# A two-layer hybrid encoder on one core: when the first weight sums of the FFN are made, who adds the squares of the norms, and what is fetched or kept for the last down projections

## The chip, the cores and the metric

The kernel runs on one core of a Trainium2 chip. The metric is the device time of one execution in microseconds (us), as the median of several runs. Engines are named as in the profile: PE multiplies matrices (its weight loads are PEld), DVE, ACT and POOL work element by element, SP issues transfers. Each engine works through its own list of instructions in order, so an instruction that waits holds up all that stand behind it on that engine. A transfer issued by POOL can add into its destination instead of overwriting it; such a one is called an adding DMA here.

## The reference

Two layers over 768 tokens of 1024 channels (256 of a prompt and 512 of a sample). Each layer is a norm, three token mixers, gates and an output projection, then a second norm and a gated FFN of 2816 channels, both with a residual:

```python
h = x + mixers(rmsnorm(x, norm1_g)) @ w_out
up = rmsnorm(h, norm2_g) @ w_up                  # 2 x 2816 columns
up = centred depthwise conv of width 3 over tokens(up)
x = h + (silu(gate half of up) * value half of up) @ w_down
```

After the second layer there is a last rmsnorm. `rmsnorm(x, g)` is `x * rsqrt(mean(x*x) + eps) * g`, with the mean over the 1024 channels of one token. All is float32.

## The kernel before

Activations lie with channels on the 128 partitions and 768 tokens along the row, as 8 tiles (m = 0 to 7) for 1024 channels. Every float32 product is three PE products of rounded parts: hi*hi, hi*lo, lo*hi. For weights, ACT makes the hi part `wh` (L320, L330) and DVE the lo part `wl` by subtracting (L349). `Stream` (object `W`) walks through a fixed list of weights and issues loads, hi and lo parts some steps ahead of their use.

**The norm is applied late.** `prep` and `layer_out` write the unnormalized values times g. The factor of a token, `rsqrt`, is found beside the products: `sumsq(x, k)` squares tile k on ACT (L487, L490) and adds it to one accumulator page, tiles 1 to 6 on POOL and 7 on DVE (both L492). `rstd_tok` sums over partitions on PE (L498, 12 products), scales on DVE (L501) and takes the power on POOL (L504). `rstd_bc` spreads the factors over all partitions: small diagonal matrices on DVE (L518), products on PE (L519), copies on ACT (L521).

**`layer_out`** computes the output projection tile by tile ("out m"). DVE adds the residual (L988) to the PSUM buffer, ACT and DVE make the hi and lo parts of three combinations for the FFN (L970, L968, L971, L991 to L998), `sumsq` follows, and POOL stores the tile to `x_mid` (L1002).

**The FFN up projection** works on 22 groups g of 128 gate and 128 value columns. Each is a two by two block product in 7 pieces instead of 8 (P1 to P7; products at L1092 into the PSUM buffers `ga` and `gb`, copies out at L1100 to L1116). Some pieces multiply sums of weight quarters `qa` to `qd`. Those sums are adding DMAs on POOL (`add`, L272): sum1 is qc += w, sum2 is qd += qc, sum3 is qb += w, sum4 is raw += qd. `load2` asks SP for qd. `Stream.acts` says at which piece each is issued, counted from the group's P1; for g = 0 the negative counts fall into the last outs. P2 of a group needs qd after sum2. The convolution, silu and product of a group (L1029 to L1072) run over the pieces that follow.

**The down projections** ("dn") take the 22 blocks in 8 chunks c0 to c7 of 2 or 3 (FFC), each for 8 tiles m. `ffn_steps` writes one order of pieces and dn steps; `TAIL` dn steps of the next to last chunk stay for after the last piece. A dn is `dense` (L425) into one of two PSUM buffers d (`dps` takes turns), then `evac`: DVE adds the residual page that SP fetched from DRAM (L1152), SP stores it. In chunk c7 of layer 0, `evac` also calls `prep` (ACT L478, DVE L479) and `sumsq` for the next layer. In layer 1, c7 is computed in two cuts of columns (512, then 256) with the weights loaded and split twice; its evacuation is L1142, and `final` then scales (L1210) and stores.

**`dense_tok`** (L538) computes a mixer's input projection with tokens on partitions: tiles 0 to 3 lie in d buffer 0, tiles 4 and 5 in buffer 1. The first one of a layer (`kouter`) runs in two halves s = 0, 1 over the channels, and in s = 0 with the channel block outside and all 6 tiles inside. Its copy out is L570 on ACT.

Pages of 128x768 come from a pool of 7 and are free again when their last reader is done.

## Time and profile before

| | |
|---|---|
| median of 3 runs | 2481.14 us (2477.6 to 2487.31) |
| profiled execution | 2487.01 us, of which the span is 2485.2 us |
| mean granted clock of PE in the span | 0.985 |
| PE busy | 2400.7 us |
| DVE busy | 1549.1 us |
| ACT busy | 1110.7 us |
| POOL busy | 297.8 us |

In a row of the trace's timeline the numbers are start (us from the span's start) and duration, then engine, line, operation, what is written and read, and in brackets how long the engine was idle before it and what it is held to have waited for. A granted clock of 1.00 means that PE ran at the higher of its two levels (2.4 GHz) throughout the stretch, 0.50 that it ran at the lower (1.2 GHz).

### The profile page before, as it was taken

The numbers are of one execution on the slowest core, as the hardware profiler recorded it, in microseconds if no ns is written. First come the engines' busy times: TensorE is split into PE (matmuls) and PEld (weight loads), VectorE is DVE, ScalarE is ACT, GpSimd is POOL, SyncE is SP. The second block draws the span as 40 slices with busy tenths as digits, with TensorE's granted clock in tenths as the row PEclk, the third lists the DMA queues.
The fourth block names the chain that finished last, engine by engine and source line by source line (L and its number), as shares of the span: only waits on it lengthen the run. The fifth ranks groups of instructions, "written<-read, shape, count | busy, mean of one in ns | idle before, by whom it ended". The sixth has DMA issues, their size and how long they took to land. (4 is left out here: it accounts for less than half of the span.)

```text
span 2485.2 us, 38816 instructions
## 1 busy us (share of the span) xinstructions
PE 2400.7 (97%) x15030; PEld 2325.9 (94%) x15030; DVE 1549.1 (62%) x2689; ACT 1110.7 (45%) x2194; POOL 297.8 (12%) x406
## 2 busy tenths in 40 slices
PE   9999999999989999999799999999999899999996
PEld 8999999899979999999799999998999899999995
DVE  5555446554648777777745554555446687777775
ACT  4344345652335444444423553466323454444442
POOL 1000110000221111111100001100003211111102
PEclk9999999999989999999999999999999999999998
DMA  4411321113358987887622113111124698878854
GB/s 146 101 58 50 53 69 52 35 35 101 123 125 228 258 239 223 229 229 211 198 86 64 50 50 71 60 43 35 43 104 136 134 271 248 241 216 245 223 168 159
DMA packets 140712, 336.12 MB, mean 135 GB/s; under 512 B 16616, under 2 KB 35176, under 8 KB 140528
## 3 DMA queue, kind: packets, MB, share of 16 engines
q1 hardware_dynamic: 109296, 265.99, 32.6%
q0 software_dynamic: 31232, 67.66, 15.3%
q8 instruction: 118, 1.93, 0.3%
q14 instruction: 66, 0.54, 0.1%
HBM read 251.79 MB, written 58.72 MB: 125 GB/s over the span
## 5 line engine op out<-in xcount | busy, mean ns | idle before, releaser
L425 PE MATMUL d<-u,wh 128*128 128x384 f32 (+2 forms) x4608 | 1024.4, 343 | 17.1 <-DVE u L1142 7.9
L425 PEld LDWEIGHTS d<-u,wh 128*128 128x128 f32 x4608 | 806.7, 189 | 37.2 <-issue 26.4
L425 PE MATMUL d<-u,wl 128*128 128x384 f32 (+2 forms) x2304 | 596.7, 338 | 0.0
L425 PEld LDWEIGHTS d<-u,wl 128*128 128x128 f32 x2304 | 421.0, 189 | 1.1
L349 DVE TENSOR_TENSOR wl<-raw,wh 128x512 fp32r<-128x512 f32 (+1 forms) x261 | 256.6, 985 | 199.0 <-ACT wh L330 159.8
L1092 PE MATMUL ga<-u,wh 128*128 128x384 f32 x1408 | 364.9, 340 | 11.7 <-ACT u L1100 7.9
L1092 PE MATMUL gb<-u,wh 128*128 128x384 f32 x1056 | 274.5, 341 | 15.7 <-ACT u L970 7.8
L1092 PEld LDWEIGHTS ga<-u,wh 128*128 128x128 f32 x1408 | 256.9, 189 | 14.5 <-ACT u L1100 8.7
L538 PE MATMUL d<-wh,u 128*128 128x256 f32 x1344 | 250.2, 286 | 11.0 <-DVE pg L1152 7.7
L1092 PE MATMUL ga<-u,wl 128*128 128x384 f32 x704 | 238.8, 339 | 0.1
L538 PEld LDWEIGHTS d<-wh,u 128*128 128x128 f32 x1344 | 212.6, 193 | 13.2 <-issue 8.0
L1092 PEld LDWEIGHTS gb<-u,wh 128*128 128x128 f32 x1056 | 193.1, 190 | 18.5 <-ACT u L970 8.4
L538 PE MATMUL d<-wl,u 128*128 128x256 f32 x672 | 191.7, 285 | 3.0 <-DVE wl L349 3.0
L330 ACT ACTIVATE wh<-raw 128x1024 fp32r<-128x1024 f32 x129 | 135.3, 1049 | 109.3 <-PE d L538 52.1
L1092 PE MATMUL gb<-u,wl 128*128 128x384 f32 x528 | 179.1, 339 | 0.0
L1152 DVE TENSOR_TENSOR pg<-d,pg 128x768 f32<-128x768 f32 x120 | 114.6, 955 | 85.9 <-PE d L425 80.8
L1029 ACT ACTIVATE pg<-u,vec 128x769 f32<-128x769 f32 x88 | 91.0, 1034 | 111.4 <-DVE u L1037 76.3
L1092 PEld LDWEIGHTS ga<-u,wl 128*128 128x128 f32 x704 | 133.3, 189 | 0.7 <-DVE wl L349 0.7
L538 PEld LDWEIGHTS d<-wl,u 128*128 128x128 f32 x672 | 129.2, 192 | 3.6 <-DVE wl L349 3.4
L636 DVE TENSOR_TENSOR u<-s,u 128x128 fp32r<-128x128 f32 (+1 forms) x112 | 36.9, 329 | 121.1 <-ACT u L635 120.9
L1092 PEld LDWEIGHTS gb<-u,wl 128*128 128x128 f32 x528 | 100.1, 190 | 0.1
L731 PE MATMUL s<-u,u 128*128 128x256 f32 (+2 forms) x384 | 99.9, 342 | 0.0
(191 smaller groups left out, 3129.1 us busy)
## 6 DMA issues: line engine op xcount, KB each, us to landing
raw<-w_pk SPq DMA_DIRECT2D x174, 512.0 KB, 3.7
pg<-xm SPq DMA_DIRECT2D x120, 384.0 KB, 5.1
xm<-pg SPq DMA_DIRECT2D x112, 384.0 KB, 3.9
u<-w_pk SPq DMA_DIRECT2D x104, 192.0 KB, 3.4
qa<-w_pk SPq DMA_DIRECT2D x44, 256.0 KB, 4.6
qb<-w_pk SPq DMA_DIRECT2D x44, 256.0 KB, 3.1
qc<-w_pk SPq DMA_DIRECT2D x44, 256.0 KB, 3.7
qd<-w_pk SPq DMA_DIRECT2D x44, 256.0 KB, 4.4
```

The lines of the kernel that those rows point to most:

```text
L330: ACT.activation(hi[:, :n], t[:, :n], AF.Copy)
L349: DVE.tensor_tensor(lo, t, fl(hi), ALU.subtract)
L425: PE.matmul(out=ps[:, h, 0:b - a], lhsT=w, rhs=x[:, a:b], start=first and i == 0 and pi == 0, stop=last and i == nk - 1 and pi == 2,)
L538: PE.matmul(out=outs[t], lhsT=x, rhs=w, start=k == 0 and pi == 0 and t % 2 == 0, stop=k == KD - 1 and pi == 2, skip_group_check=True)
L636: DVE.tensor_tensor(u[:, 1, a:b], ps, fl(u[:, 0, a:b]), ALU.subtract)
L731: PE.matmul(out=ps[:, 0:w], lhsT=q, rhs=kb[:, c, lo * P:hi * P], start=c == 0, stop=c == 1)
L1029: ACT.activation(f, h[:, 1:770], AF.Identity, scale=cw(1, ct), bias=vec[:, VCB + ct:VCB + ct + 1])
L1092: PE.matmul(out=o, lhsT=a[:, w], rhs=x[:, b], start=p in ("P1", "P2", "P5") and kp == 0 and pi == 0, stop=kp == 3 and pi == 2, skip_group_ ...
L1152: DVE.tensor_tensor(h2(xa), ps[:, :, 0:384], h2(xa), ALU.add)
```

## The change

Seven edits: (1) all four quarters of group 0 are loaded at the start of `layer_out`, and sum1 and sum2 of group 0 are issued there; for later groups load2, sum1, sum2 and sum4 come one or two pieces earlier, with two buffers for qd. (2) For all norms but the first of the kernel, `sumsq` keeps two accumulators (even and odd tiles), adds squares 2 to 5 by adding DMAs, 6 and 7 on DVE, and joins the accumulators on DVE at k = 6. (3) `rstd_tok` comes one piece later, `rstd_bc` two. (4) One dn of the next to last chunk goes to just before the last group's P4. (5) After the last piece, residual pages are asked for two tiles ahead instead of one. (6) The lo and hi weights of layer 1's last chunk stay on chip for its second cut. (7) `dense_tok` with `kouter` takes the d buffers in turn and does tiles 0 to 3 first, then 4 and 5.

```diff
-TAIL = 4
+TAIL = 5
@@ ffn_steps
     for g, p in seq:
+        if (g, p) == (NJ - 1, "P4"):
+            r.append(("dn", todo[0][0], todo.pop(0)[1], (0, HT, T)))
         r.append(("pc", g, p))
@@ Stream.__init__
-                    for k, f in ((-2, self.load2), (-2, self.sum1), (-1, self.sum2), (0, self.sum3), (4, self.sum4)):
-                        at = j + k if e[2] == 0 and k < 0 else pcs[i + k]
-                        self.acts.setdefault(at, []).append((f, e[1], e[2]))
+                    for k, f in ((-4, self.load2), (-3, self.sum1), (-2, self.sum2), (0, self.sum3), (3, self.sum4)):
+                        if e[2] or k >= 0:
+                            self.acts.setdefault(pcs[i + k], []).append((f, e[1], e[2]))
@@ Stream.quart
-            t = ph["sb"].tile([P, 512], F32, tag="q" + k, name=nm("q" + k))
+            t = ph["sb"].tile([P, 512], F32, tag="q" + k, name=nm("q" + k), bufs=2 if k == "d" else 1)
@@ Stream.split
-                if self.open is None:
+                if e[:3] == ("down", DEPTH - 1, len(FFC) - 1):
+                    k = None
+                    if e[3] % 2 == 0:
+                        st["keep"] = unit()
+                    h, l2 = (st["keep"][:, e[3] % 2, i * HT:i * HT + w] for i in range(2))
+                elif self.open is None:
@@ sumsq
-    def sumsq(x_ap, k, dve=False):
+    def sumsq(x_ap, k, dve=None):
         n = x_ap.shape[-1]
-        if k == 0:
-            st["acc"] = page()[:, 0:n]
-            ACT.activation(st["acc"], x_ap, AF.Square)
+        c = k % 2 if dve is None else 0
+        if k == c:
+            st["acc", c] = page()[:, 0:n]
+            ACT.activation(st["acc", c], x_ap, AF.Square)
+            return
+        sq = page()[:, 0:n]
+        ACT.activation(sq, x_ap, AF.Square)
+        if dve is not None or k >= KD - 2:
+            (POOL if dve is False else DVE).tensor_tensor(st["acc", 0], st["acc", 0], sq, ALU.add)
+            if dve is None and k == KD - 2:
+                DVE.tensor_tensor(st["acc", 0], st["acc", 0], st.pop(("acc", 1)), ALU.add)
         else:
-            sq = page()[:, 0:n]
-            ACT.activation(sq, x_ap, AF.Square)
-            eng = DVE if dve or k == KD - 1 else POOL
-            eng.tensor_tensor(st["acc"], st["acc"], sq, ALU.add)
+            POOL.dma_start(out=st["acc", c], in_=sq, accum_op=ALU.add)
@@ dense_tok
-        d = [dps(0), dps(1)]
+        d = [dps(), dps()] if kouter else [dps(0), dps(1)]
...
-                order = [(kk, t) for kk in range(4) for t in range(NT)]
+                order = [(kk, t) for ts in (range(4), range(4, NT)) for kk in range(4) for t in ts]
@@ layer_out
-        W.quart("a", l)
-        W.quart("b", l)
-        W.quart("c", l)
+        for k in "abcd":
+            W.quart(k, l)
...
         fetch(1)
+        W.sum1(l, 0)
+        W.sum2(l, 0)
@@ layer_ffn
-                if s[1] == 0 and s[2] == "P6":
+                if (s[1], s[2]) == (0, "P5"):
                     rstd_tok()
-                elif s[1] == 0 and s[2] == "P7":
+                elif (s[1], s[2]) == (1, "P1"):
                     rstd_bc(gap=True)
                 elif s[1] == NJ - 1 and s[2] == "P3":
+                    deep = 3
...
-            for _, c2, m2, _ in downs[0:2]:
+            for _, c2, m2, cuts2 in downs[0:deep]:
```

The order of instructions shows the first place on DVE, at out 7 of layer 0: the addition of out 7's residual into `u` and, ahead of it, the lo part of group 0's `qd`. Before:

```order
L971 SCALAR_TENSOR_TENSOR u_6615<-u_6180,vec_91,u_6615 128x384
L992 TENSOR_TENSOR pg_6618<-pg_6616 128x384
L971 SCALAR_TENSOR_TENSOR u_6615<-pg_6618,u_6615 128x384
L349 TENSOR_TENSOR wl_6692<-qd_6619,wh_6691 128x512
L988 TENSOR_TENSOR u_6180<-d_6694,u_6180 128x768
```

The same place in the changed kernel (line numbers there are 8 to 17 higher: L504 and L506 are the two additions of `sumsq`, L357 is L349, L1005 is L988):

```order
L988 SCALAR_TENSOR_TENSOR u_6618<-u_6182,vec_91,u_6618 128x384
L1009 TENSOR_TENSOR pg_6621<-pg_6619 128x384
L988 SCALAR_TENSOR_TENSOR u_6618<-pg_6621,u_6618 128x384
L504 TENSOR_TENSOR pg_6258<-pg_6258,pg_6686 128x768
L506 TENSOR_TENSOR pg_6258<-pg_6258,pg_6326 128x768
L357 TENSOR_TENSOR wl_6692<-qd_6177,wh_6691 128x512
L1005 TENSOR_TENSOR u_6182<-d_6694,u_6182 128x768
```

Two additions (of out 6's square and of the odd accumulator) have come in ahead of out 7's residual; the odd accumulator is the one into which the last adding DMA, of out 5, goes. The second place is POOL from out 5 of layer 0 to the power of `rstd_tok` (L504 before, L520 after), with the stores of the outs (`xm`) and the sums. Before:

```order
L492 TENSOR_TENSOR pg_6254<-pg_6254,pg_6609 128x768
L1002 DMA xm_210<-u_6179 128x768
L272 DMA qc_6175<-w_pk 128x512
L492 TENSOR_TENSOR pg_6254<-pg_6254,pg_6686 128x768
L1002 DMA xm_211<-u_6180 128x768
L272 DMA qd_6619<-qc_6175 128x512
L1002 DMA xm_212<-u_6180 128x768
L1018 MEMSET u_6762 128x2 x3
L1018 MEMSET u_6766 128x2 x3
L272 DMA qb_6173<-w_pk 128x512
L504 TENSOR_TENSOR sm_6836<-sm_6834,neghalf 128x6
```

After (L508 is the adding DMA of `sumsq`, L274 a weight sum):

```order
L508 DMA pg_6326<-pg_6612 128x768
L1019 DMA xm_210<-u_6181 128x768
L1019 DMA xm_211<-u_6182 128x768
L1019 DMA xm_212<-u_6182 128x768
L1035 MEMSET u_6762 128x2 x3
L1035 MEMSET u_6766 128x2 x3
L274 DMA qb_6173<-w_pk 128x512
L274 DMA qc_6781<-w_pk 128x512
L274 DMA raw_6504<-qd_6177 128x512
L274 DMA qd_6790<-qc_6781 128x512
L520 TENSOR_TENSOR sm_6857<-sm_6855,neghalf 128x6
```

Group 0's sum1 and sum2 are gone from here (they stand at the start of the output projection), and three more sums now stand ahead of the power: sum1 and sum2 of group 1 and sum4 of group 0. The third place is DVE in the last chunk of layer 0, at m = 6 and m = 7, each with its residual (L1152 before, L1168 after) and its scaled tile (L479, L489). Before:

```order
L1152 TENSOR_TENSOR pg_11654<-d_11688,pg_11654 128x768
L479 SCALAR_TENSOR_TENSOR u_11712<-pg_11654,vec_11368,u_11712 128x768
L349 TENSOR_TENSOR wl_11719<-raw_11294,wh_11718 128x1024
L1152 TENSOR_TENSOR pg_11683<-d_11721,pg_11683 128x768
L479 SCALAR_TENSOR_TENSOR u_11745<-pg_11683,vec_11368,u_11745 128x768
L492 TENSOR_TENSOR pg_11523<-pg_11523,pg_11748 128x768
```

After:

```order
L1168 TENSOR_TENSOR pg_11624<-d_11687,pg_11624 128x768
L489 SCALAR_TENSOR_TENSOR u_11711<-pg_11624,vec_11368,u_11711 128x768
L504 TENSOR_TENSOR pg_11525<-pg_11525,pg_11714 128x768
L506 TENSOR_TENSOR pg_11525<-pg_11525,pg_11558 128x768
L357 TENSOR_TENSOR wl_11719<-raw_11283,wh_11718 128x1024
L1168 TENSOR_TENSOR pg_11655<-d_11721,pg_11655 128x768
L489 SCALAR_TENSOR_TENSOR u_11745<-pg_11655,vec_11368,u_11745 128x768
L504 TENSOR_TENSOR pg_11525<-pg_11525,pg_11748 128x768
```

The two additions of tile 6 stand ahead of tile 7's residual, where POOL added before.

## Rows read from the trace of the kernel before

**Rows 1.** The page, busy us (share of the span) and instructions of an engine.

```profile
PE 2400.7 (97%) x15030; PEld 2325.9 (94%) x15030; DVE 1549.1 (62%) x2689; ACT 1110.7 (45%) x2194; POOL 297.8 (12%) x406
```

**Rows 2.** Stretch, us; busy us of PE, PEld, DVE, ACT, POOL; granted clock; DMA.

```profile
680.00:720.00 40.00, 29.80 (x147) 28.22 (x146) 18.11 (x31) 12.21 (x23) 11.55 (x18) 0.83 0.43 105
...
1200.00:1250.00 50.00, 38.18 (x216) 37.04 (x215) 31.53 (x30) 19.88 (x26) 12.33 (x8) 0.90 0.69 223
...
1900.00:1950.00 50.00, 40.15 (x218) 38.26 (x217) 23.50 (x39) 16.32 (x29) 13.45 (x20) 0.90 0.51 127
```

**Rows 3.** Waits of PE over the span: us in total, times, longest.

```profile
PE d L425 <- DVE u L1142: 7.9, 6, 2.6
PE ga L1092 <- ACT u L1100: 7.9, 2, 4.1
PE gb L1092 <- ACT u L970: 7.8, 2, 4.0
PE d L538 <- DVE pg L1152: 7.7, 1, 7.7
```

**Rows 4.** DVE, ACT and POOL at layer 0's FFN start: start, us, instruction, [idle before].

```profile
693.71 0.69 DVE L349 TENSOR_TENSOR wl<-qd,wh 128x512 fp32r<-128x512 f32 x1 [7.07 <-ACT wh L320]
694.32 0.95 DVE L988 TENSOR_TENSOR u<-d,u 128x768 f32<-128x768 f32 x1
...
678.49 0.83 ACT L490 ACTIVATE pg<-u 128x768 f32<-128x768 f32 x1
...
693.05 0.63 ACT L320 ACTIVATE wh<-qd 128x512 fp32r<-128x512 f32 x1 [6.25 <-DMA qd<-qc]
...
701.58 0.47 ACT L1100 ACTIVATE u<-ga 128x384 f32<-128x384 f32 x1
...
689.31 0.89 POOL L272 DMA_DIRECT2D qd<-qc  x1
```

**Rows 5.** DMA issues at 640:700: count, KB each, median us to landing.

```profile
qd<-qc POOLq DMA_DIRECT2D x1, 256.0 KB, 3.7
```

**Rows 6.** PE in the stretch of outs, busy us of L425 alone.

```profile
640.00:689.00 49.00, 48.83 (x278) 48.51 (x277) 1.00 0.45 140
```

**Rows 7.** PE at layer 0's FFN start.

```profile
702.10 1.01 PE L1092 MATMUL ga<-u,wh 128*128 128x384 f32 x2 [4.12 <-ACT u L1100]
...
715.67 0.68 PE L519 MATMUL d<-dg,ones 128*128 128x128 f32 x4 [1.39 <-DVE dg L518]
```

**Rows 8.** ACT and PE at the third column group, layer 0.

```profile
742.68 0.63 ACT L320 ACTIVATE wh<-qd 128x512 fp32r<-128x512 f32 x1 [3.95 <-DMA qd<-qc]
...
749.45 0.98 PE L1092 MATMUL gb<-u,wh 128*128 128x384 f32 x2 [3.32 <-DVE u L1102]
```

**Rows 9.** POOL's issues of sums beside the second group's load.

```profile
719.60 0.85 POOL L272 DMA_DIRECT2D qd<-qc  x1 [7.16 <-DMA qd<-w_pk]
```

**Rows 10.** DVE, POOL and PE at the end of layer 0.

```profile
1210.60 0.56 DVE L349 TENSOR_TENSOR wl<-u,wh 128x384 fp32r<-128x384 f32 x1
...
1219.19 1.99 DVE L349 TENSOR_TENSOR wl<-u,wh 128x384 fp32r<-128x384 f32 x1
...
1218.90 1.86 POOL L492 TENSOR_TENSOR pg<-pg,pg 128x768 f32<-128x768 f32 x1 [3.14 <-ACT pg L490]
...
1222.19 0.94 PE L425 MATMUL d<-u,wh 128*128 128x384 f32 x4 [1.64 <-DVE pg L1152]
...
1241.40 0.55 PE L538 MATMUL d<-wh,u 128*128 128x256 f32 x1 [7.70 <-DVE pg L1152]
```

**Rows 11.** PE in that product's first half, busy us of L538 alone.

```profile
1241.00:1252.50 11.50, 11.10 (x71) 11.13 (x72) 0.72 0.58 166
1247.50:1252.50 5.00, 5.00 (x44) 5.00 (x44) 1.00 0.35 108
```

**Rows 12.** ACT, evacuation of tiles 4 and 5 after that product.

```profile
1262.73 0.84 ACT L570 ACTIVATE u<-d,sm 128x256 f32<-128x256 f32 x2 [1.14 <-PE d L538]
```

**Rows 13.** DVE in the last chunk of layer 1.

```profile
2435.80 1.40 DVE L349 TENSOR_TENSOR wl<-u,wh 128x384 fp32r<-128x384 f32 x1 [1.11 <-ACT wh L320]
```

More of the change, by code (lines that the diff above doesn't have):

```diff
@@ L69, in plan @@
                 r.append(("pc", l, s[1], s[2]))
-            else:
+            elif s[3][0] == 0:
                 r.append(("down", l, s[1], s[2]))
@@ L184, in small @@
     def small(w):
-        return sm.tile([P, w], F32, tag=f"sm{w}", name=nm("sm"))
+        return sm.tile([P, w], F32, tag=f"sm{w}", name=nm("sm"), bufs=3 if w == 24 else 6)
     def h2(ap):
@@ L216, in __init__ @@
             self.nd = 0
+            self.src = {}
             for i, (kind, j, e) in enumerate(loads()):
+                if kind == "y":
+                    self.src[e[1], e[2], "22"] = w_d[i, :, 512:1024]
                 if kind == "x":
+                    self.src[e[1], e[2], "11"] = w_d[i, :, 0:512]
                     for k in "abcd":
@@ L223, in __init__ @@
             self.quarter = {}
-            self.src = {}
             self.acts = {}
@@ L241, in load @@
             if e[0] == "pc":
-                self.src[e[1], e[2], "22"] = w_d[i, :, 512:1024]
                 self.quarter[e[1], e[2], "12"] = t[:, 0:512]
@@ L256, in quart @@
             self.quarter[e[1], e[2], {"a": "11", "b": "21", "c": "s1", "d": "s2"}[k]] = t
-            if k == "a":
-                self.src[e[1], e[2], "11"] = w_d[i, :, 0:512]
         def load_down(self, l):
@@ L332, in split @@
             self.at[j] = k
-            self.live.setdefault(k, set()).add(j)
+            if k is not None:
+                self.live.setdefault(k, set()).add(j)
             if parts > 1:
@@ L354, in done @@
             k = self.at[j]
+            if k is None:
+                return
             self.live[k].discard(j)
@@ L481, in prep @@
             sumsq(x_ap, k)
-    def sumsq(x_ap, k, dve=False):
+    def sumsq(x_ap, k, dve=None):
         n = x_ap.shape[-1]
-        if k == 0:
-            st["acc"] = page()[:, 0:n]
-            ACT.activation(st["acc"], x_ap, AF.Square)
-        else:
-            sq = page()[:, 0:n]
-            ACT.activation(sq, x_ap, AF.Square)
-            eng = DVE if dve or k == KD - 1 else POOL
-            eng.tensor_tensor(st["acc"], st["acc"], sq, ALU.add)
+        c = k % 2 if dve is None else 0
+        if k == c:
+            st["acc", c] = page()[:, 0:n]
+            ACT.activation(st["acc", c], x_ap, AF.Square)
+            return
+        sq = page()[:, 0:n]
[4 more added lines that the diff above has]
+                DVE.tensor_tensor(st["acc", 0], st["acc", 0], st.pop(("acc", 1)), ALU.add)
+        else:
+            POOL.dma_start(out=st["acc", c], in_=sq, accum_op=ALU.add)
     def rstd_tok(n=NT):
-        acc = st.pop("acc")
+        acc = st.pop(("acc", 0))
         ps = sps()
@@ L1130, in fetch_last @@
         def fetch_last(m):
-            for k in range(m, min(m + 2, KD)):
-                if k not in seen:
-                    seen.add(k)
-                    nc.sync.dma_start(out=st["xu"][k // 2][:, k % 2], in_=x_mid[k])
+            if m not in seen:
+                seen.add(m)
+                nc.sync.dma_start(out=st["xu"][m // 2][:, m % 2], in_=x_mid[m])
         def evac(c, m, cuts, ps):
@@ L1160, in layer_ffn @@
         downs = [s for s in steps if s[0] == "dn"]
+        deep = 2
+        kept = {}
         for s in steps:
@@ L1163, in layer_ffn @@
                 piece(s[1], s[2])
-                if s[1] == 0 and s[2] == "P6":
+                if (s[1], s[2]) == (0, "P5"):
                     rstd_tok()
-                elif s[1] == 0 and s[2] == "P7":
+                elif (s[1], s[2]) == (1, "P1"):
                     rstd_bc(gap=True)
                 elif s[1] == NJ - 1 and s[2] == "P3":
+                    deep = 3
                     if l < DEPTH - 1:
                         load_vec(l + 1)
+                    else:
+                        st["xu"] = [unit(F32) for _ in range(4)]
                 continue
@@ L1175, in layer_ffn @@
             final_ = last and l == DEPTH - 1
-            if c == len(FFC) - 2 and m == KD - 1 and l == DEPTH - 1:
-                st["xu"] = [unit(F32) for _ in range(4)]
-            for _, c2, m2, _ in downs[0:2]:
+            for _, c2, m2, cuts2 in downs[0:deep]:
                 if not (c2 == len(FFC) - 1 and l == DEPTH - 1):
                     fetch(c2, m2)
-                elif cuts[0] == 0:
+                elif cuts2[0] == 0:
                     fetch_last(m2)
@@ L1185, in layer_ffn @@
                 tick()
-            hi, lo = W.get(("down", l, c, m))
+            if cuts[0] == 0:
+                hi, lo = W.get(("down", l, c, m))
+                if final_:
+                    kept[m] = hi, lo
+            else:
+                hi, lo = kept[m]
             ps = dps()
```

## The prediction

> **What bounds the kernel now.** First the page, for the share of each engine: PE is busy for 2400.7 us of a span of 2485.2 [rows 1], so the products themselves leave little; what can be won are the 85 us in which PE stands and stretches where its clock is low. Then busy time by stretch, to find where PE stands: from 680 to 720 (layer 0's FFN start) it works 29.8 of 40 us, from 1200 to 1250 (end of layer 0) 38.2 of 50, from 1900 to 1950 (layer 1's FFN start) 40.2 of 50, and the granted clock there is 0.83 to 0.90, so for part of each stretch PE runs at the lower of its two levels [rows 2]. Then PE's list of waits, to name what ends last there: ACT L1100, which frees the buffer for P6 (7.9 us in two, one per layer), ACT L970, which makes what P2 reads (7.8 in two), DVE L1152 ahead of layer 1's first mixer product (7.7 in one), DVE L1142 in the last chunk (7.9 in six) [rows 3]. The seven edits fall on these edges and on the order of the sums, so I cost them edge by edge.
>
> **A. Layer 0's FFN start.** Look at DVE: the lo part of `qd` starts at 693.71 after 7.07 us of idling, and only behind it comes out 7's residual, L988, at 694.32. DVE idled for ACT's hi part at 693.05, and that for the DMA qd<-qc, which POOL had issued at 689.31 [rows 4] and which landed in 3.7 us [rows 5]. A late sum holds up an evacuation that does not read it. PE's outs run without a gap until 689 (48.83 of 49 us) [rows 6]; with the sum made at the start of the outs, L988 can begin then, at 689.0, 5.3 us earlier. The chain behind it to L1100 keeps its length of 701.58 - 694.32 = 7.26 us [rows 4], and P6 follows by 0.5: 696.8, where it was 702.10 [rows 7]. P1 and P2, some 4 us of products from 689, still end before that, so a wait of nearly 4 us stays and the clock may fall in it again, after less standing than before.
>
> Two additions now stand on DVE ahead of L988, and they need the adding DMA of out 5. A square such as ACT's at 678.49 ends at 679.3 [rows 4]; with an issue of 0.9 on POOL and the 3.7 us of the nearest adding DMA [rows 5] it lands near 684, and 687 would do. So they cost nothing here as long as issue and landing stay under 7.6 us together.
>
> The 1.39 us ahead of L519 [rows 7] should go, since a whole piece now lies between, but the power of `rstd_tok` stands behind three sums on POOL, and one of these (sum2 of group 1) waits for another's landing: 0 to 2 us of it come back. With a shorter stay at the lower clock I take 6 in all (4.5 to 8).
>
> At the third group PE waits 3.32 us for L1102; ACT's hi part of `qd` at 742.68 was late by 3.95 for its DMA [rows 8], and a little earlier POOL had stood 7.16 us until a load of qd landed before it could issue sum2 [rows 9]. load2 comes two pieces earlier, sum1 and sum2 one, and a second buffer spares the load the wait for the last reader. Moved by more than they are late, they take away the 3.3 and some of the slower clock behind it: 4 (2 to 5).
>
> **B. The end of layer 0.** The period of a tile is POOL's 3.14 + 1.86 = 5.0 us, of which PE stands 1.64. While POOL's L492 runs (1218.90 to 1220.76), DVE's L349 takes 1.99 us; at 1210.60, with POOL still, it took 0.56 [rows 10]. Without additions on POOL the period falls by those 1.43 us to 3.6. Three tiles gain 1.4 each, the last two, with wider splits, I put at 0.9 each; DVE gets 1.9 us of additions after tile 6; asking for pages earlier should gain 1.5 ahead of tile 0. Tile 7's residual, which ran until just before 1241.4, so starts near 1234.7 instead of 1240.3, and tile 6's near 1228.7. Edit 7 gives the first four tiles of the next product the buffer of tile 6: L538 starts near 1229.7 instead of 1241.40 [rows 10]. Its first 48 products at 5.0 / 44 = 0.114 us are 5.5; the other 24 wait for tile 7 (1235.6) and end near 1238.5. Before, 71 products took until 1252.5 at a mean clock of 0.72 [rows 11]. That is 14 us earlier. Against it, the product after that begins in the buffer where tiles 4 and 5 now are emptied last, by an L570 of 0.84 us [rows 12]: 1.0 with PE's start, and some for pages, since two accumulators and squares in flight hold more of the 7, and a residual page may have to wait until an adding DMA has landed. Net 12.5 (9 to 14).
>
> **C. Layer 1's FFN start.** The same two waits have nearly the same lengths (7.9 and 7.8 us in two each) [rows 3] and the stretch is as empty [rows 2]: 5.8 (4.5 to 7).
>
> **D. The end of layer 1.** L349 takes 1.40 us where POOL adds [rows 13], 0.56 where not [rows 10], so DVE's period falls by 0.84 and most of PE's 7.9 us of waits for L1142 [rows 3] could go; in the second cut L349 and L320 are gone. But there tiles come faster than an adding DMA lands: the square of tile 5 goes into the accumulator that tile 3's is still on its way to, and tile 7's evacuation stands behind both on DVE. I take 3.5 (0 to 6); each us by which a landing exceeds 3.7 costs 2 here.
>
> **E. The first mixer product.** There tiles 4 and 5 are also emptied last: the 1.0 of B again, a loss. Its new order of tiles costs nothing as long as PE waits for the first weights anyway; if not, a few tenths.
>
> Edit 4 I put at nothing (0 to 0.8): the dn only changes place within products that run without a gap.
>
> **A rule weighed.** POOL's issues of sums took 0.85 and 0.89 us [rows 4, 9], one of them while DVE stood idle and one beside DVE's work, so DVE does not seem to hold up an issue. The Trainium skill, "SBUF — State Buffer", section "SBUF: two separate sides", says that a DMA issued from POOL can be left without descriptors while a DVE instruction holds the port pair that the two share. By the figure on that page (some 2.5 us more for such a DMA), an estimate, D would lose 5 and the sum would be 25.8.
>
> **Sum.** 6 + 4 + 12.5 + 5.8 + 3.5 - 1.0 = 30.8 us off the profiled 2487.0: 2456.2. The median of the runs shown is lower than that execution by 2481.14 / 2487.01, which gives 2450.4; I forecast 2450.5. All terms at their low ends give 19 off, at their high ends 39.
>
> **The rivals.** *Only the layer ends gain.* At both FFN starts a new wait takes the place of the old one: the power behind POOL's sums, or L988 behind an odd accumulator that lands late. A's 6 and C's 5.8 shrink to 1 together: 20 off, 2461. For it: three sums ahead of the power, and a wait for a landing of 7.16 us on POOL [rows 9]. Against: the power is also wanted later by a piece. Chance 0.17.
>
> *Issues held up by DVE.* If an issue has to sit out the DVE instructions then running (0.6 to 2 us each in [rows 4, 10], say two or three, 3 us), adding DMAs land after 6.7 us: D loses 6 and B 1, so 24 off, 2457. The issue times above speak against it. The rule of the Trainium skill ("SBUF — State Buffer") weighed above is of this kind. Chance 0.12.
>
> *Landings that gate DVE: slower than before.* Edit 2 rests on one time, that of an adding DMA, because DVE's list now waits for it ahead of out 7 in both layers, ahead of tile 7 in layer 0, and in each cut of the last chunk. A late us costs 2 from 3.7 on (D), 1.5 from about 6 (B), 2 from 7.6 (A and C together). At 10 us that is 12.6 + 6 + 4.8, so 7 of the 30.8 are left; near 11.5 the sign turns, and at 14, 2494, it is 0.5% slower. The nearest row has 3.7 us for two thirds of the data [rows 5]; by size alone that would be at most 5.6. Chance 0.05, and 0.06 for a milder form that ends at 2469 to 2481.
>
> *More than I think*: the clock stays up through the FFN starts and D is worth 6: 42 off, 2439. Chance 0.05.
>
> **Numbers.** The forecast itself holds 0.55. 0.5% here is 12.4 us, about what a measurement of this kernel can tell from no change. Faster by more: 0.55 + 0.17 + 0.12 + 0.05, less 0.02 for the first two rivals falling short, 0.87. Same 0.08, slower 0.05. The range is 2440 (terms near their high ends) to 2467 (the two rivals with gains, and low ends of the other terms); it leaves out the last two cases.
>
> **What would show it.** Right: L1005 (L988 before) within 1 us of out 7's last product, and P6's wait for L1117 (L1100) the only long one of PE there; no 128x384 L357 (L349) over 1 us at the layer ends; the first L554 (L538) of layer 1 some 12 us earlier against the last piece; no waits for L1158 (L1142) in the first cut. Wrong: L506 starting late with PE behind it; POOL's power L520 late with PE's L535 (L519) behind; a residual page late because an adding DMA holds one.

## The result, and the profile of the changed kernel

The changed kernel takes 2449.59 us in the median of 4 runs (2445.58 to 2454.07), the kernel before 2480.64 (2477.6 to 2487.31): a ratio of 0.987, with a 95% interval of 0.984 to 0.990. The forecast was 2450.5, with a range of 2440 to 2467. The profiled execution took 2452.3 us (span 2450.1) against 2487.01, 34.7 less. Between the medians it is 31.1, and 30.6 were forecast. The total came out as forecast, but not by the terms forecast: the FFN starts gave more, the end of layer 0 less.

Line numbers of the changed kernel are higher: L1005 is L988 of before, L1117 is L1100, L357 is L349, L514 is L498, L535 is L519, L1168 and L1158 are L1152 and L1142, L554 is L538, L586 is L570, L504 and L506 are the additions of `sumsq` on DVE and L508 its adding DMA.

The page, busy us of PE, which answers to [rows 1]:

```profile
PE 2393.8 (98%) x15030; PEld 2325.3 (95%) x15030; DVE 1531.0 (62%) x2691; ACT 1106.6 (45%) x2186; POOL 268.2 (11%) x396
```

PE's list of waits, which answers to [rows 3] (us in total, times, longest):

```profile
PE ga L514 <- DVE pg L504: 8.8, 2, 5.2
PE ga L1109 <- ACT u L1117: 7.2, 2, 3.6
...
PE d L554 <- DVE pg L1168: 3.2, 1, 3.2
...
PE d L554 <- ACT u L586: 1.9, 2, 0.9
```

The waits for ACT L970 (7.8 us) are gone from the list, those for L1100, now L1117, remain. L554 waits 3.2 where L538 waited 7.7. New at the head stands the norm of the last chunk, L514, behind DVE's L504: 8.8 us in two. The two waits of L554 for L586, one in each layer, are the price of edit 7, 0.93 us each.

The FFN start of layer 0 in the changed kernel, on DVE, POOL and PE, which answers to [rows 4, 7]:

```profile
684.08 0.96 DVE L506 TENSOR_TENSOR pg<-pg,pg 128x768 f32<-128x768 f32 x1
684.96 0.68 DVE L357 TENSOR_TENSOR wl<-qd,wh 128x512 fp32r<-128x512 f32 x1
687.05 0.96 DVE L1005 TENSOR_TENSOR u<-d,u 128x768 f32<-128x768 f32 x1 [1.41 <-PE d L435]
...
703.67 0.85 POOL L274 DMA_DIRECT2D qd<-qc  x1 [3.09 <-DMA qc<-w_pk]
704.23 1.66 POOL L520 TENSOR_TENSOR sm<-sm,neghalf 128x6 f32<-128x6 f32 x1
...
694.84 1.01 PE L1109 MATMUL ga<-u,wh 128*128 128x384 f32 x2 [3.60 <-ACT u L1117]
...
707.41 0.68 PE L535 MATMUL d<-dg,ones 128*128 128x128 f32 x4
```

L506, L357 and then L1005 follow each other without a wait for a transfer; L1005 now waits 1.41 us for PE's product, as forecast. P6 still waits 3.60 us for L1117. POOL's power L520 had to wait behind a sum for 3.09, but PE has no wait ahead of the first products of L535, where it had one of 1.39.

Busy us by stretch (columns as in [rows 2]), first one more row of before, then the same of the changed kernel:

```profile
690.00:760.00 70.00, 55.03 (x274) 51.54 (x273) 37.86 (x64) 27.79 (x53) 13.99 (x23) 0.88 0.52 120
```

```profile
690.00:760.00 70.00, 65.26 (x361) 63.94 (x360) 49.69 (x85) 37.45 (x74) 15.29 (x18) 0.95 0.70 157
```

From 690 to 760 PE now works 65.3 of 70 us instead of 55.0, and the granted clock is 0.95 instead of 0.88. From out 7's last product to the fourth down projection of the layer (stretch A of the table below) PE stands 4.7 us instead of 15.2, and its 432 products take 77.9 us instead of 83.1: 10.5 us of waits and 5.2 of clock.

The end of layer 0, on ACT, DVE and PE, which answers to [rows 10]:

```profile
1212.51 0.84 ACT L502 ACTIVATE pg<-pg 128x768 f32<-128x768 f32 x1 [1.99 <-DMA sp<-pg]
1213.26 1.04 ACT L337 ACTIVATE wh<-raw 128x1024 fp32r<-128x1024 f32 x1
...
1201.66 0.56 DVE L357 TENSOR_TENSOR wl<-u,wh 128x384 fp32r<-128x384 f32 x1
...
1214.33 1.23 DVE L357 TENSOR_TENSOR wl<-raw,wh 128x1024 fp32r<-128x1024 f32 x1 [2.76 <-ACT wh L337]
1215.48 0.95 DVE L1168 TENSOR_TENSOR pg<-d,pg 128x768 f32<-128x768 f32 x1
...
1220.26 0.96 DVE L506 TENSOR_TENSOR pg<-pg,pg 128x768 f32<-128x768 f32 x1 [0.94 <-DMA pg<-pg]
...
1216.57 0.55 PE L554 MATMUL d<-wh,u 128*128 128x256 f32 x1 [3.21 <-DVE pg L1168]
```

The split L357 of 128x384 takes 0.55 to 0.56 us in every tile, as forecast. But ACT's square of tile 5 waits 1.99 us until a store of a page has landed, the hi part L337 stands behind it, DVE waits 2.76 us for that hi part, and tile 6's residual L1168 stands behind the split, so L554 starts 3.21 us late. Tile 7's residual stands behind L506, which waits 0.94 us for an adding DMA.

The first cut of layer 1's last chunk, on POOL, DVE and PE, which answers to [rows 13]:

```profile
2403.12 0.85 POOL L508 DMA_DIRECT2D pg<-pg  x1 [50.02 <-PE d L435]
...
2409.91 0.85 POOL L508 DMA_DIRECT2D pg<-pg  x1 [3.62 <-DMA pg<-pg]
...
2413.29 0.69 DVE L504 TENSOR_TENSOR pg<-pg,pg 128x512 f32<-128x512 f32 x1 [3.30 <-DMA pg<-pg]
2414.85 0.69 DVE L506 TENSOR_TENSOR pg<-pg,pg 128x512 f32<-128x512 f32 x1 [0.86 <-DMA pg<-pg]
...
2417.63 1.87 PE L514 MATMUL ga<-ones,pg 128*128 128x2 f32 x8 [5.19 <-DVE pg L504]
```

Tile 4's adding DMA waits 3.62 us on POOL until tile 2's has landed in the same accumulator (issued at 2403.12, it took 6.3 us); L504 waits for tile 4's and L506 for tile 5's; PE waits 5.19 us ahead of the norm, where before it had waited 3.27:

```profile
2451.93 1.60 PE L498 MATMUL ga<-ones,pg 128*128 128x2 f32 x8 [3.27 <-DVE pg L492]
```

All adding DMAs of `sumsq` in the changed kernel, from the view of their line (issues with shortest, median and longest ns; us to landing, shortest, median, longest):

```profile
L508 POOL DMA_DIRECT2D pg<-pg x20: 842/852/893, 650.0 to 2434.7; - x20
...
DMA to landing us min/median/max: 2.6/4.3/6.6
```

### The profile page after: what moved, and what is told of

It is laid out like the page before. It is cut to its first block, busy times and chain, and to the rows that moved or that the text cites. A ratio compares the mean times of both kernels' runs of the same rounds, so it can differ in the third digit from the quotient of the medians.

```text
span 2450.1 us, 38743 instructions
## 1 busy us (share of the span) xinstructions
PE 2393.8 (98%) x15030; PEld 2325.3 (95%) x15030; DVE 1531.0 (62%) x2691; ACT 1106.6 (45%) x2186; POOL 268.2 (11%) x396
## 4 chain that ended last, share of the span: by engine, by line
PE 85%; DMA 5%; DVE 3%; ACT 3%; issue 3%; POOL 0%; SPq 0%; POOLq 0%; DVEq 0%; ACTq 0%
PE d L435 46%; PE ga L1109 13%; PE gb L1109 9%; PE d L554 7%; PE s L799 3%; PE s L786 3%; PE s L747 3%; DMA raw<-w_pk 1%; DMA pg<-gqk 1%; PE s L659 1%; DMA qd<-qc 1%; DVE wl L357 1%; DMA qc<-w_pk 0%; DMA u<-w_pk 0%; ACT wh L327 0%
## 5 line engine op out<-in xcount | busy, mean ns | idle before, releaser
L435 PE MATMUL d<-u,wh 128*128 128x384 f32 x4512 | 996.6, 342 | 5.4 <-ACT pg L1074 5.0
L435 PEld LDWEIGHTS d<-u,wh 128*128 128x128 f32 x4512 | 788.1, 188 | 20.3 <-issue 11.0
L435 PE MATMUL d<-u,wl 128*128 128x384 f32 x2256 | 579.5, 338 | 0.0
L435 PEld LDWEIGHTS d<-u,wl 128*128 128x128 f32 x2256 | 410.7, 188 | 0.0
L357 DVE TENSOR_TENSOR wl<-raw,wh 128x512 fp32r<-128x512 f32 (+1 forms) x261 | 248.1, 951 | 200.9 <-ACT wh L337 155.4
L554 PE MATMUL d<-wh,u 128*128 128x256 f32 x1344 | 249.1, 285 | 7.5 <-DVE pg L1168 3.2
L554 PEld LDWEIGHTS d<-wh,u 128*128 128x128 f32 x1344 | 211.4, 191 | 9.7 <-issue 3.5
L554 PE MATMUL d<-wl,u 128*128 128x256 f32 x672 | 190.8, 284 | 2.0 <-DVE wl L357 2.0
L337 ACT ACTIVATE wh<-raw 128x1024 fp32r<-128x1024 f32 x129 | 135.3, 1050 | 103.3 <-PE d L554 47.6
L1168 DVE TENSOR_TENSOR pg<-d,pg 128x768 f32<-128x768 f32 x120 | 114.6, 955 | 90.8 <-PE d L435 85.6
L554 PEld LDWEIGHTS d<-wl,u 128*128 128x128 f32 x672 | 128.6, 191 | 2.6 <-DVE wl L357 2.4
```

The lines of the kernel that those rows point to most:

```text
L337: ACT.activation(hi[:, :n], t[:, :n], AF.Copy)
L357: DVE.tensor_tensor(lo, t, fl(hi), ALU.subtract)
L435: PE.matmul(out=ps[:, h, 0:b - a], lhsT=w, rhs=x[:, a:b], start=first and i == 0 and pi == 0, stop=last and i == nk - 1 and pi == 2,)
L554: PE.matmul(out=outs[t], lhsT=x, rhs=w, start=k == 0 and pi == 0 and t % 2 == 0, stop=k == KD - 1 and pi == 2, skip_group_check=True)
L1168: DVE.tensor_tensor(h2(xa), ps[:, :, 0:384], h2(xa), ALU.add)
```

## The experiments

One execution of a kernel differs from another by several us (2445.6 to 2454.1 for the same code), so the runs are compared by four stretches of each trace that lie between the same PE instructions: **A** from out 7's last product to the fourth down projection of layer 0, **C** the same in layer 1, **B** from the last piece of layer 0 to the first `rstd_tok` of layer 1, **D** from the last piece of layer 1 to the last product. Times in us, from the starts and ends of those rows:

| kernel | A | B | C | D | execution |
|---|---|---|---|---|---|
| before | 98.3 | 68.5 | 93.1 | 68.2 | 2487.0 |
| changed | 82.6 | 60.8 | 84.1 | 65.3 | 2452.3 |
| u_sums0 | 84.8 | 59.0 | 87.3 | 63.5 | 2454.1 |
| u_squares | 83.5 | 62.6 | 84.1 | 59.9 | 2450.3 |
| u_both | 88.3 | 62.7 | 89.7 | 60.6 | 2461.7 |
| u_rstd | 87.2 | 56.5 | 86.1 | 64.9 | 2453.7 |
| u_sumsg | 86.6 | 58.9 | 89.0 | 64.0 | 2461.0 |
| u_qd | 88.2 | 59.0 | 90.2 | 63.3 | 2463.6 |
| u_kouter | 81.7 | 65.5 | 85.0 | 63.7 | 2454.3 |
| u_deep | 81.6 | 58.6 | 84.3 | 65.1 | 2450.1 |
| c_cut1 | 82.9 | 57.8 | 83.0 | 62.7 | 2442.6 |
| b_cuts | 82.0 | 59.6 | 84.3 | 61.1 | 2442.1 |
| b_late | 82.0 | 55.9 | 83.8 | 63.9 | 2448.1 |
| b_all | 81.7 | 56.7 | 83.9 | 59.4 | 2441.9 |

The spread of unchanged code can be read off: A is 81.6 to 82.9 (mean 82.1) and C 83.0 to 85.0 (84.1) in the seven kernels that leave the FFN start as changed, B is 56.5 to 60.8 (mean 58.8) in the seven that leave layer 0's end as changed, D is 63.3 to 65.3 (mean 64.2) in the eight that leave the last chunk. In B 4 us of spread are nothing but that. The kernel before and every other kernel were profiled once, so a difference in the table that is not well over these spreads shows nothing. The executions hold more that is in no stretch: in layer 0's mixers the same product waits between nothing and 2.75 us in these traces, 0.42 in the changed kernel's.

**First sums late again (u_sums0).**

```diff
-        for k in "abcd":
+        for k in "abc":
             W.quart(k, l)
...
-        W.sum1(l, 0)
-        W.sum2(l, 0)
...
+                    if e[2] == 0:
+                        for k, f in ((-2, self.load2), (-2, self.sum1), (-1, self.sum2)):
+                            self.acts.setdefault(j + k, []).append((f, e[1], e[2]))
```

> The changed kernel with one part undone: the load of qd and the first two sums of group 0 are issued at outs 6 and 7 again, in both layers. Theory (the late sum held up out 7's residual): DVE's residual of out 7 waits 4 to 6 us again behind the lo part of qd, PE waits for ACT's hi part and again for P1's copy, and with the lower clock each layer gives back 5 to 7 us: about 2461 against 2450. Rival (the gain at the FFN starts comes from rstd_tok and rstd_bc standing later and from the sums of the later groups): at most 2 us per layer come back, 2452 to 2454.

A and C lost 2.7 and 3.2 us against the means of the unchanged, 82.1 and 84.1: the theory's mechanism with half of its size. DVE and POOL at out 7 (L360 is the split, L1006 the residual):

```profile
692.23 0.69 DVE L360 TENSOR_TENSOR wl<-qd,wh 128x512 fp32r<-128x512 f32 x1 [4.71 <-ACT wh L330]
692.84 0.95 DVE L1006 TENSOR_TENSOR u<-d,u 128x768 f32<-128x768 f32 x1
...
688.18 0.85 POOL L277 DMA_DIRECT2D qd<-qc  x1 [5.16 <-DMA qc<-w_pk]
```

The residual stands behind the split again, but DVE idles 4.71 us instead of 7.07: POOL could issue the sum at 688.18, as soon as sum1 had landed.

**Squares by POOL again (u_squares).**

```diff
-        c = k % 2 if dve is None else 0
+        c = 0
...
+        (DVE if dve or k == KD - 1 else POOL).tensor_tensor(st["acc", 0], st["acc", 0], sq, ALU.add)
...
-            POOL.dma_start(out=st["acc", c], in_=sq, accum_op=ALU.add)
```

> The changed kernel with the squares added as before: tiles 1 to 6 by POOL, 7 by DVE, one accumulator, no adding DMA. Theory (POOL's additions slow DVE's subtractions in the last chunks): the period of a tile in the last chunk of layer 0 is 5.0 us again instead of 3.6, the split 1.4 us longer, and the first mixer product of layer 1 starts 5 to 8 us later against the last piece; in layer 1's last chunk PE waits 0.8 us per tile in the first cut again, but the 5.2 us ahead of the first cut's norm fall to about 3.3, so that place is even within 2. In all 2456 to 2459. Rival (landings of the adding DMAs cost as much as POOL's additions did): within 3 us of 2450.

The theory missed the sum, and the rival held. B lost 3.8 us against the mean of 58.8, A 1.4, C nothing, and D *won* 4.3 against the mean of 64.2: the whole kernel is as fast as the changed one. PE at the end of layer 0 and ahead of the first norm of the last chunk (L509 is L514):

```profile
1213.81 0.93 PE L435 MATMUL d<-u,wh 128*128 128x384 f32 x4 [1.62 <-DVE pg L1163]
...
2419.81 1.05 PE L509 MATMUL ga<-ones,pg 128*128 128x2 f32 x8 [1.24 <-DVE pg L503]
```

In layer 0 PE waits 1.62 us per tile again, as in [rows 10]. In layer 1 the wait of 5.19 us is 1.24. So edit 2 is worth some 5 us in B and A together, and costs 4 in the last chunk. (B's 62.6 is outside the spread of 56.5 to 60.8, and u_both, without edit 2 either, has 62.7.)

**Both undone (u_both).** The diffs of the two runs above together.

> The changed kernel with two parts undone at once: the late first sums of group 0 and POOL's additions of squares. Undoing one alone cost 2 to 3 us per FFN start (sums) and about 1 (squares). Theory (each holds the sum up by itself: POOL issued the sum of qd behind its addition of out 6's square, so either edit alone brings most of the gain): together they cost clearly more than the two alone, 5 to 7 us per FFN start, and out 7's residual waits some 5 us on DVE again. Rival (they add up): 3 to 4 us per FFN start, and DVE waits 2 to 3 us.

A lost 6.2 and C 5.6, where the two alone lose 2.7 + 1.4 in A and 3.2 + 0 in C. DVE and POOL at out 7:

```profile
694.90 0.69 DVE L360 TENSOR_TENSOR wl<-qd,wh 128x512 fp32r<-128x512 f32 x1 [7.07 <-ACT wh L330]
...
688.13 1.83 POOL L506 TENSOR_TENSOR pg<-pg,pg 128x768 f32<-128x768 f32 x1 [4.16 <-ACT pg L505]
...
690.49 0.89 POOL L277 DMA_DIRECT2D qd<-qc  x1
```

DVE waits 7.07 us, as in [rows 4]: the sum of qd (690.49) is issued only after POOL has added out 6's square (1.83 us) and stored the tile, and that addition waits for its square. Each edit takes one of the two things away that made the sum late: of the 6.2 and 5.6 us the early sum alone brings 4.8 and 5.6 (u_squares), the edit of the squares alone 3.5 and 2.4 (u_sums0).

**`rstd_tok` and `rstd_bc` at their old places (u_rstd).**

```diff
-                if (s[1], s[2]) == (0, "P5"):
+                if (s[1], s[2]) == (0, "P6"):
...
-                elif (s[1], s[2]) == (1, "P1"):
+                elif (s[1], s[2]) == (0, "P7"):
```

> The changed kernel with rstd_tok and rstd_bc one and two pieces earlier, as before. Theory (their wait was real and is now covered): ahead of the first product of rstd_bc PE waits 1.4 us or more again in each layer, 1 to 3 us per layer with the clock, because the power now stands behind more sums on POOL. Rival (no matter): within 0.5 us per layer.

The wait of 1.39 us ahead of L535 is back in both layers, but A lost 5.1 and C 2.0. The rest is clock: the same products take 81.1 us in A, where they take 76.8 to 78.2 in the seven kernels that leave the FFN start as changed, and 79.6 in C, where they take 76.9 to 78.3. PE in the ten us after P6's start, busy by stretch (columns as in [rows 2]), and its row of `rstd_tok`, first in u_rstd:

```profile
697.00:707.00 10.00, 9.88 (x35) 9.89 (x36) 3.99 (x8) 2.69 (x7) 3.90 (x6) 0.50 0.49 131
```

```profile
701.12 2.55 PE L514 MATMUL d<-ones,pg 128*128 128x2 f32 x12
```

and in u_deep, where the place is as in the changed kernel:

```profile
697.00:707.00 10.00, 9.22 (x49) 9.22 (x50) 4.76 (x9) 3.36 (x8) 2.19 (x3) 0.83 0.64 157
```

```profile
703.46 1.40 PE L514 MATMUL d<-ones,pg 128*128 128x2 f32 x12
```

With the twelve products right behind P6, the granted clock stays at 0.50 over the ten us; with a whole piece in between, it is 0.83, and the same twelve products take 1.40 us instead of 2.55. In layer 1 of u_rstd it is the same (0.54, and 2.55 us). In the kernels with the later place the clock of these ten us is 0.69 to 0.86 and the twelve take 1.39 or 1.40, in both layers of all twelve. But the kernel before, with the early place, has 2.55 us in layer 0 and this in layer 1, where the clock of the ten us was 0.81:

```profile
1933.60 1.39 PE L498 MATMUL d<-ones,pg 128*128 128x2 f32 x12
```

So the early place went with the low clock in three of four cases, not in all.

**Later groups' sums at their old pieces (u_sumsg), and one buffer for qd (u_qd).**

```diff
-                    for k, f in ((-4, self.load2), (-3, self.sum1), (-2, self.sum2), (0, self.sum3), (3, self.sum4)):
+                    for k, f in ((-2, self.load2), (-2, self.sum1), (-1, self.sum2), (0, self.sum3), (4, self.sum4)):
...
-            t = ph["sb"].tile([P, 512], F32, tag="q" + k, name=nm("q" + k), bufs=2 if k == "d" else 1)
+            t = ph["sb"].tile([P, 512], F32, tag="q" + k, name=nm("q" + k), bufs=1)
```

> The changed kernel with load2, sum1, sum2 and sum4 of groups 1 to 21 at their old pieces (qd keeps two buffers). Theory (the later waits at the third group, 3.3 us in layer 0 and 2.9 in layer 1, went because the sums start earlier): PE waits 2 to 4 us for L1119 at the third group again in each layer, 3 to 5 us per layer with the clock. Rival (the second buffer of qd alone removed them): within 1 us per layer.

> The changed kernel with one buffer for qd instead of two. Theory (the second buffer alone removed the waits at the third group, 3.3 us in layer 0 and 2.9 in layer 1, since moving the sums back to their old pieces did not bring them back): PE waits 2 to 4 us for L1119 at the third group again, 3 to 8 us longer in all. Rival (they went because the groups before are no longer late): no such wait, within 2 us.

Both cost 4.5 to 6.1 us in A and 4.9 to 6.1 in C, and both expectations missed the place. ACT and PE in u_sumsg:

```profile
708.73 0.63 ACT L327 ACTIVATE wh<-raw 128x512 fp32r<-128x512 f32 x1 [2.69 <-DMA raw<-qd]
...
710.43 0.68 PE L535 MATMUL d<-dg,ones 128*128 128x128 f32 x4 [2.88 <-DVE dg L534]
```

POOL in u_qd:

```profile
707.26 0.85 POOL L274 DMA_DIRECT2D qd<-qc  x1 [6.97 <-DMA qd<-w_pk]
707.82 1.66 POOL L520 TENSOR_TENSOR sm<-sm,neghalf 128x6 f32<-128x6 f32 x1
```

At layer 0's third group no wait for L1119 beyond 0.5 us came back. PE stood 2.88 us (u_sumsg) and 3.77 us (u_qd) ahead of L535 instead: in u_sumsg because group 0's sum4, now behind the power on POOL, kept a hi part waiting, and behind that the split and the diagonal matrices on DVE; in u_qd because the sum ahead of the power waited 6.97 us for the load of qd. Late sums cost about the same wherever they are met first; which of the two parts took away the 3.3 us at the third group stays open, because with either undone PE arrives there later. In u_qd the middle of each FFN is longer too: between A and the last piece lie 404.5 us, and 404.3 in layer 1, where u_sumsg has 400.3 and 399.4.

**Old buffers and order of the first mixer product (u_kouter).**

```diff
-        d = [dps(), dps()] if kouter else [dps(0), dps(1)]
+        d = [dps(0), dps(1)]
-                order = [(kk, t) for ts in (range(4), range(4, NT)) for kk in range(4) for t in ts]
+                order = [(kk, t) for kk in range(4) for t in range(NT)]
```

> The changed kernel with the first mixer product of a layer in its old buffers and order (all six tiles inside each channel block, tiles 4 and 5 in buffer 1). Theory (that product had to wait for tile 7's evacuation): at layer 1's start it begins about 6.7 us later, after tile 7's residual; the two waits of 0.93 us for the copies of tiles 4 and 5 go, and some of the lower clock is paid either way: 3 to 5 us longer, 2453 to 2455. Rival (the new order only moves the wait): within 1 us, or 2 us shorter by the two waits.

B lost 6.7 us against the mean, and PE's row shows where:

```profile
1222.49 0.55 PE L554 MATMUL d<-wh,u 128*128 128x256 f32 x1 [8.82 <-DVE pg L1168]
```

8.82 us for tile 7's residual. The two waits of 0.93 us went, so edit 7 is worth near 5 in all. It was the larger part of B, where edit 2 brought 3.8.

**The residual one tile ahead in layer 0 (u_deep).**

```diff
-                    deep = 3
+                    deep = 3 if l == DEPTH - 1 else 2
```

> The changed kernel with the residual asked for one tile ahead, as before, in layer 0 only. Theory (of 7 pages one too few: a square waits for a page, and behind it on ACT a hi part, on DVE tile 6's residual, on PE the first product of layer 1): ACT's squares of tiles 4 and 5 no longer wait for a store, tile 6's residual starts 2 to 3 us earlier against the last piece, and 2 to 4 us are gained with the clock, 2446 to 2448. Rival (pages are not short, the early request is what keeps DVE fed): DVE waits 1 to 2 us per tile for a residual page and 2 to 5 us are lost.

DVE at tiles 6 and 7, and PE's first mixer product behind them:

```profile
1213.24 1.23 DVE L357 TENSOR_TENSOR wl<-raw,wh 128x1024 fp32r<-128x1024 f32 x1 [0.69 <-ACT wh L337]
...
1220.30 0.96 DVE L506 TENSOR_TENSOR pg<-pg,pg 128x768 f32<-128x768 f32 x1 [2.07 <-DMA pg<-pg]
...
1215.48 0.36 PE L554 MATMUL d<-wh,u 128*128 128x256 f32 x1 [1.43 <-DVE pg L1168]
...
1223.32 0.39 PE L554 MATMUL d<-wh,u 128*128 128x256 f32 x1 [1.89 <-DVE pg L1168]
```

The square no longer waits for a page, and the split ahead of tile 6 waits 0.69 us instead of 2.76. L554 waits 1.43 us instead of 3.21 for tile 6. But L506 then waits 2.07 for its adding DMA, tile 7's residual stands behind it, and L554 waits 1.89 for that in the middle of its product. B is 58.6, the mean of the unchanged, so the 2 to 4 us expected did not come: without the wait for a page PE waits at the next tile, and nothing is won that can be told from the spread.

**The last chunk without adding DMAs: DVE in both cuts (c_cut1), DVE in the first and POOL in the second (b_cuts).**

```diff
         n = x_ap.shape[-1]
+        if dve is None and n < T:
+            dve = True
         c = k % 2 if dve is None else 0
```

In b_cuts the added assignment is `dve = n > HT or k == KD - 1`.

> The changed kernel with the squares of layer 1's last chunk (both cuts) added by DVE into one accumulator, without adding DMAs; everything else as it is. Theory (the chained landings are the 5.2 and 3.6 us ahead of the two norms there, and DVE has room while it waits 1.1 us per tile for ACT's hi part): the waits ahead of L514 fall to about 1.5 each, and the stretch after the last piece is 5 to 7 us shorter: 2443 to 2445. Rival (DVE becomes the bound of the first cut): PE waits 0.3 to 0.8 us per tile there and at most 2 us are won.

> The changed kernel with the squares of layer 1's last chunk added by DVE in the first cut and by POOL (tiles 1 to 6) and DVE (7) in the second, without adding DMAs. Theory (each cut has its own free engine: in the first DVE waits for hi parts and POOL would slow its splits; in the second nothing is split, and DVE is busy with the scaling of the first cut): the first cut is as short as with DVE alone (37.0 us from the last piece to the first norm) and the second as with POOL alone (18.4 between the norms), so the stretch after the last piece is 58 to 60 us instead of 65.3; about 2443. Rival (the second cut was short there only because the first ended late): the second stays at 21 to 22 us, and the stretch at 62.

DVE and PE in the first cut of c_cut1 (L506 is the addition, L516 the norm):

```profile
2393.76 0.69 DVE L506 TENSOR_TENSOR pg<-pg,pg 128x512 f32<-128x512 f32 x1 [0.70 <-ACT pg L504]
2394.36 0.55 DVE L357 TENSOR_TENSOR u<-u,u 128x384 fp32r<-128x384 f32 x1
...
2408.00 1.67 PE L516 MATMUL ga<-ones,pg 128*128 128x2 f32 x8 [1.87 <-DVE pg L506]
```

DVE's addition stands where DVE had waited for the hi part; a tile takes 2.5 us, where it took 2.3, and PE waits 1.87 us ahead of the norm instead of 5.19. From the last piece to the first norm it takes 37.0 us instead of 38.0 to 40.0 in the eight traces of the code as changed. The second cut stayed at 22.5 us with DVE and came to 21.1 with POOL (19.7 in b_all), not the 18.4 of u_squares; b_all has b_cuts' code there, so whether the rival was right for the second cut is not settled. D is 62.7 and 61.1, 1.5 and 3.1 less than the mean of 64.2: c_cut1 did not bring the 5 to 7 us expected, and its 2442.6 us are lower than that mostly by what other stretches happened to take.

**The join after tile 7 (b_late), and all together (b_all).** b_late is u_deep with the join of the two accumulators moved in the last chunk of layer 0, where `join` is `KD - 1` (elsewhere `KD - 2`):

```diff
-            if dve is None and k == KD - 2:
+            if dve is None and k == join:
```

> The changed kernel with two edits at the end of layer 0: the residual asked for one tile ahead, and the two accumulators joined after tile 7's residual instead of before. Theory (the join stands on DVE ahead of tile 7's residual and waits there for an adding DMA): PE's second wait in the first mixer product (1.9 us with the residual one tile ahead) goes, and from the last piece to the norm of layer 1 it takes 55 to 57 us, where five runs of the changed order took 56.4 to 60.8. Rival (tile 7 is late for its split and its product, not for the join): 58 to 60.

> The edits of b_cuts and b_late together. If they add: 5 to 7 us from the last chunk of layer 1 and 1 to 3 from the end of layer 0 off the changed kernel's 2449.6, so 2440 to 2444, a ratio to the kernel before of 0.983 to 0.985. If the gains are lost in the spread of the stretches between: 2446 to 2450.

b_late has the shortest B, 55.9, as expected, but u_rstd reached 56.5 without the edit, so it is not shown to help. b_all takes 2441.86 us in the median of 5 runs (2441.12 to 2444.14) against 2483.12 of the kernel before on the same chip: ratio 0.983 (0.981 to 0.985), where the changed kernel has 0.987 (0.984 to 0.990). The intervals just touch. That is what was expected if the two add; of the 7.7 us between the medians D has its share with 59.4, where the eight traces of the unchanged chunk have 63.3 to 65.3, and B's 56.7 lies within the spread.

## Why the prediction was right, and where it was not

The reading of the profile held: the four stretches at the edges that PE's waits named hold 35.5 us of gain, and the executions differ by 34.7. That the total came so near is luck: terms erred to both sides. Profiled execution against profiled execution:

- **A: 10 forecast, 15.7 measured; C: 5.8 forecast, 9.1 measured.** Mechanism right, size off. The start of L1005 at the end of out 7's product and the remaining wait of about 4 us for L1117 came as forecast. Too small was what the prediction called the shorter stay at the lower clock: 5.2 us in A instead of the one to two that the two sums left for it. u_rstd shows that part of this hangs on edit 3, which the prediction costed only by its wait of 1.39 us. In C the clock gave only 0.9 us and the waits 8.1 (14.1 to 6.0); there a wait of the kernel before at layer 1's third group had been left out of the sum, and 0.89 us of it are left:

```profile
1972.01 0.59 PE L1092 MATMUL gb<-u,wh 128*128 128x384 f32 x2 [2.85 <-DVE u L1102]
```

- **In A the cause of the late sum was read as half of what it was.** The prediction blamed where sum2 was asked for. POOL's addition of a square ahead of it did nearly as much: each undone alone costs 0 to 3 us per layer, both 6.
- **B: 12.5 forecast, 6.7 measured** (7.7 in the stretch, less the 1.0 of L586 that was forecast). Two steps failed. The product's start was forecast 41.3 us after the last piece (1229.7 - 1188.4), and came after 45.3. Some 1.5 of these 4 us were lost because the granted clock was low after PE's wait of 2.48 us for L1074, where it had been 1.00 after the same wait of before (the ten us, first of the changed kernel, then of before):

```profile
1180.00:1190.00 10.00, 9.87 (x48) 9.90 (x49) 6.43 (x10) 2.29 (x6) 0.00 (x0) 0.83 0.85 295
```

```profile
1197.00:1207.00 10.00, 9.77 (x56) 9.80 (x57) 6.53 (x11) 2.39 (x6) 0.00 (x0) 1.00 0.90 317
```

  The rest lies in the wait of 3.21 us for tile 6's residual; with no wait for a page 1.43 of it stayed (u_deep). And the clock was low again in the first half of the product, which the prediction had at the higher level: from L554's start to the norm it took 15.6 us as before, not 13.3 as in u_rstd, where it stayed up. The period itself fell to 3.6 us as worked out. The clock here is in part chance: u_rstd has the same code in this stretch and the same wait of 2.48 us, its clock is 1.00 all through B, and B is 12.1 us shorter than before, 11.1 without the 1.0. In the mean of the seven it is 9.7 shorter, 8.7 without it. The forecast of 12.5 was for the better case.
- **D: 3.5 forecast, 3.0 measured.** Here the rival that was priced, landings that gate DVE, is what limits the gain. The other edits with POOL's additions (u_squares) bring 8.3 us; edit 2 with its adding DMAs takes 4 to 5 of them back. What of the 8.3 is the kept weights and what the earlier pages no run separates. The price of 2 us per us of landing was of the right kind, but was only asked for beyond 3.7 us; what the landings cost up to that stood in the sum only as the choice of 3.5 out of PE's 7.9 us of waits.
- **E: -1.0 forecast, a wait of 0.93 us for L586 measured** in layer 0, besides the one of layer 1 that was counted under B. What the new order costs or gains there in all no run shows.
- **Edit 4 was put at 0 to 0.8:** the stretch between A and the last piece is 401.3 before and 400.3 in the later runs (u_qd apart), and layer 1 gains the same 0.9 to 1.0. The products there did not run without a gap, as the prediction had it: before, PE waited in each layer ahead of the last piece, and that wait is gone.

```profile
1183.94 0.62 PE L1092 MATMUL ga<-u,wh 128*128 128x384 f32 x2 [0.76 <-ACT u L1108]
```

  No run undoes edit 4 alone, nor edit 6, nor the number of buffers of small tiles with 24 columns (3 instead of 6), which the change also has and its list leaves out.
- **The rule weighed.** POOL's issues of adding DMAs took 842 to 893 ns in all 20, and landed after 2.6 to 6.6 us, 4.3 in the median. The median is within what the prediction took as the most by size, 5.6; three of the 20 took longer (6.3 to 6.6). The Trainium skill's rule ("SBUF — State Buffer", "SBUF: two separate sides") about POOL's DMAs waiting for DVE decided nothing here.
- **The slower rival** would have needed landings near 11.5 us; none took over 6.6. (At 14 us its own prices give 2496 rather than 2494; nothing hangs on that.)
- **The signs named ahead.** Those for being right came, but for the size of one: the first L554 of layer 1 stood 7.7 us earlier against the last piece, not some 12. One sign of being wrong came too: in the first cut of the last chunk L504 and L506 were late for landings, and PE behind them.

Some of the difference between the two profiles is chance: the kernel before had 1.9 us of wait and a spell of lower clock in layer 0's mixers, where the changed one's trace has 0.42 us of wait and no such spell, and the changed one had two waits of 1.1 and 2.1 us in the middle of the FFNs that no other run of this order of sums and buffers has.

## What to carry to other kernels

Where work in one engine's in-order list is late, ask for every instruction that stood ahead of it: here a sum was late for two reasons, and taking away either one brought from 2.4 to 5.6 of some 6 us, so neither run alone would have shown both causes. An addition moved from an engine to an adding DMA frees the engine but puts a landing of 2.6 to 6.6 us where there were 1 to 2 us of work; here that gained where tiles came every 3.6 us, and lost where they came about every 2.3 us and two had to follow each other into the same accumulator. A wait taken off PE was worth its length and sometimes the slow products behind it (5.2 us in A, 0.9 in C), so price the clock from rows, in both directions, and with a range.

## What the runs showed that was not expected

With `rstd_tok`'s twelve products right behind the first piece after PE's long wait, PE's granted clock stayed at 0.50 to 0.54 for ten us and the twelve took 2.55 us, in three of the four places with that order; with one more piece ahead of them it was 0.69 to 0.86 and the twelve took 1.40. Moving them and `rstd_bc` was worth 2 to 5 us per layer, of which 1.39 is the wait ahead of `rstd_bc`. The same code with the same wait of 2.48 us in B was followed by a clock of 1.00 in one trace and by some us at the lower level in another. The adding DMAs took between 2.6 and 6.6 us to land: the four of 128 KB 2.6 to 3.3, but those of 384 KB 4.0 to 6.6, the longest where tiles followed each other every 3.6 us at the end of layer 0.
